# Rank scatter of 8 x 2,048 rows: 256 rows a batch copied from HBM to HBM by two more queues, in place of passing through SBUF

## The chip, the cores and the metric

The kernel runs on one core of a Trainium2 chip. The metric is device time in microseconds. Three runs of the kernel before took 800.44, 800.96 and 801.1 us, median 800.96. One execution was also recorded by the hardware profiler; all views below come from it.

## The reference

The input `x` has 8 batches of 2,048 rows, each of 2,560 float32 values (10,240 bytes). For each batch, 2,048 scores give every row its rank, and row i goes to output row rank(i):

```python
order = np.argsort(scores, axis=1)
ranks = np.argsort(order, axis=1)
out[b_idx, ranks, :] = x
```

So 167.8 MB are read, 167.8 MB are written, and the only arithmetic is the counting of ranks.

## The kernel before, in words

**Ranks.** The rank of a score is the number of smaller scores in its batch, plus the number of equal ones at an earlier index. The scores come in as 8 rows of 2,048 (L114). TensorE transposes them into columns of 128 (L156, `s_col`), so that one column holds one score per partition; for each batch it also broadcasts the 2,048 scores to all partitions (`broadcast`, L177, into PSUM), and VectorE copies them to `s_all` (L215). VectorE then goes through the columns (`count`, L231 to L259): one instruction counts smaller scores from the group's first column on (L246), one counts smaller or equal ones in the columns before the group (L250), one counts equal ones within the group under a mask (L255). All three carry line L237 in the profile. Two additions (L263, L269) and a conversion to integers (L286, `rank_i`) make the ranks of a group.

**Groups.** `GROUPS` (L55) lists groups of rows of a batch as (first row, rows per partition m, direct). Before, there are four groups of 512 rows, m = 4, none direct. `ORDER` (L56) is the order in which VectorE and the bulk queue take them. `BULK` (L59) lists all (batch, group) pairs that aren't direct: 32 before.

**Bulk path.** A group is loaded into one of four SBUF buffers by one DMA (`load`, L105, issued at L108; 128 partitions, m rows each, one contiguous run of m x 10,240 bytes per partition), and written by m indirect DMAs (L340), each of which scatters one row of every partition to the row that `rank_i` names. The first four loads are issued by SP (L115). All else goes through the Pool queue in one hand-written order (L326): for entry k, wait for the scatters of entry k-2, issue the load of entry k+2 into its buffer, wait for the load of k and for its ranks, issue the m scatters.

**Direct path.** The code has a second path, which with the groups of before has no work (`todo`, L292, is empty). For a direct group, TensorE transposes the ranks into a row (L279) and VectorE turns them into byte offsets, (rank + b x 2048) x 10,240, in `rows_i` (`rows_out`, L195); this is done only after the next group's two additions (L273), so that VectorE does not wait for TensorE. SP and ACT take the direct columns in turn (L297). For each column of 128 rows the engine waits for the offsets (L299), loads 16 offsets at a time into registers (L301), and issues one DMA per row, from the row of `x` in HBM straight to its row of the output in HBM (L312), each adding 16 to a semaphore of that engine. At the end SP and ACT wait for all of them (L318). Neither engine has other work after the first loads.

All waits are placed by hand (`Line`); within one engine, instructions run in the order of the code.

Of the kernel before, what the change touches and what calls it, by code (L numbers as in the profile page):

```python
# [40 lines left out]
def kernel(  # L41
# [10 lines left out]

    GROUPS = [(0, 4, False), (512, 4, False), (1024, 4, False), (1536, 4, False)]  # L55
    ORDER = [0, 1, 2, 3]  # L56
    MMAX = max(m for _, m, _ in GROUPS)
    MBULK = max(m for _, m, direct in GROUPS if not direct)
    BULK = [(b, g) for b in range(B) for g in ORDER if not GROUPS[g][2]]  # L59
    NBUF = 4  # L60
    G = 16

    def first_col(g):
        return GROUPS[g][0] // P

# [23 lines left out]
    with tc.tile_critical():  # L89
# [15 lines left out]
        def load(line, k, sem):  # L105
            b, g = BULK[k]
            r, m, _ = GROUPS[g]
            line.eng.dma_start(  # L108
# [42 lines left out]
        pe.after(pl, t_ident)  # L151
        for g, (r, m, _) in enumerate(GROUPS):
            for j in range(m):
# [56 lines left out]
        for b in range(B):  # L210
# [11 lines left out]
            dve.after(dve, t_copied)  # L222
            for g in ORDER:
                r, m, direct = GROUPS[g]
# [63 lines left out]
        if pending is not None:  # L288
# [3 lines left out]
        todo = [  # L292
            (b, g, j) for b in range(B) for g in ORDER if GROUPS[g][2]
            for j in range(GROUPS[g][1])
# [88 lines left out]
```

## Time and profile before

| | before |
|---|---|
| median of 3 runs | 800.96 us |
| the profiled execution | 801.1 us |
| its span, first to last instruction | 799.3 us |
| VectorE busy | 426.3 us, all of it before about 440 us |
| POOL busy | 142.7 us |
| TensorE busy | 29.5 us |
| 128 scatters, each | 0.95 us to issue (median), 40.7 us from issue to landing |
| 28 loads by Pool, each | 0.56 us to issue, 36.1 us from issue to landing |

A span is the time from the first to the last instruction of the execution. The page cuts it into 40 equal slices and gives each engine's busy share in tenths (9 is 90% or more); DMA is the mean share of the core's 16 DMA engines. A queue's share is the time that its packets took, as part of 16 engines' span. The chain that ended last is followed back from the last instruction, at each step to what released it. A row of a tile view gives the shortest, median and longest duration in ns, then the first and last start in us. A packet is the unit in which a DMA engine moves data; the trace records start, queue, duration and size of each.

### The profile page before, as it was taken

What the parts mean: (1) busy time and instruction counts of PE and PEld (TensorE: products, weight loads), DVE (VectorE), ACT (ScalarE), POOL (GpSimd) and SP (SyncE); (2) the same over time, 40 slices, a digit from 0 to 9 for tenths busy, and PEclk for the clock granted to TensorE, in tenths of its full rate; (3) what the DMA queues carried; (4) which work ended last, traced back from release to release, by engine and by line L of the source; (5) the groups of instructions that cost most, each with busy time, mean ns of one, the idle gap of its engine ahead of it and who ended that gap; (6) DMA issues with size and microseconds to landing.
All of it is one profiled execution on the core that took longest, in us unless ns stands there. A gap on an engine that the chain in (4) does not pass through costs nothing.

```text
span 799.3 us, 1452 instructions
## 1 busy us (share of the span) xinstructions
PE 29.5 (4%) x144; PEld 26.6 (3%) x144; DVE 426.3 (53%) x834; POOL 142.7 (18%) x165
## 2 busy tenths in 40 slices
PE   3001000010010010100000000000000000000000
PEld 3001000010010010100000000000000000000000
DVE  6999999999999999999998000000000000000000
POOL 1302222102222012220222201222111222104100
PEclk9555555555555555555555555555555555555555
DMA  9999999999999999999999999999999999999993
GB/s 378 427 414 448 397 431 431 444 422 423 419 432 431 439 425 409 425 434 435 421 427 422 437 430 434 426 422 430 437 441 424 425 424 434 434 440 423 420 429 154
DMA packets 23066, 335.71 MB, mean 420 GB/s; under 512 B 2568, under 2 KB 2568, under 8 KB 2568
## 3 DMA queue, kind: packets, MB, share of 16 engines
q0 software_dynamic: 22464, 314.58, 92.5%
q1 hardware_dynamic: 592, 21.04, 6.3%
q14 instruction: 9, 0.07, 0.0%
q8 instruction: 1, 0.02, 0.0%
HBM read 167.84 MB, written 167.77 MB: 420 GB/s over the span
## 4 chain that ended last, share of the span: by engine, by line
DMA 54%; DVE 34%; POOL 4%; issue 3%; PE 1%; POOLq 0%; SPq 0%
DMA out_dram<-x,rank_i 49%; DVE trash L237 31%; DMA x<-in_x_dram 4%; POOL out_dram L340 4%; DVE s_all L215 2%; POOL x L108 1%; PE ps_all L177 0%; DVE rank L263 0%; DVE rank L269 0%; DVE rank_i L286 0%; DMA s_in<-in_scores_dram 0%; PE ps_col L156 0%; POOLq L28 0%; DVE s_col L164 0%; SPq L378 0%
## 5 line engine op out<-in xcount | busy, mean ns | idle before, releaser
L237 DVE TENSOR_SCALAR_CACHE_REDUCE trash<-s_all,s_col 128x1536 bf16<-128x1536 f32 (+3 forms) x224 | 312.4, 1426 | 0.3
L340 POOL DMA_INDIRECT out_dram<-x,rank_i x128 | 124.2, 970 | 91.8 <-issue 37.8
L108 POOL DMA_DIRECT2D x<-in_x_dram x28 | 15.8, 564 | 526.1 <-DMA out_dram<-x,rank_i 279.6
L237 DVE SCALAR_TENSOR_TENSOR trash<-s_all,s_col,mask 128x512 bf16<-128x512 f32 x128 | 95.9, 749 | 0.0
L177 PE MATMUL ps_all<-ident,s_col 128*128 128x128 f32 x128 | 27.5, 404 | 303.0 <-DVE s_all L215 302.6
L177 PEld LDWEIGHTS ps_all<-ident,s_col 128*128 128x128 f32 x128 | 24.6, 216 | 305.5 <-DVE s_all L215 305.0
L215 DVE COPY s_all<-ps_all 128x512 f32<-128x512 f32 x32 | 20.2, 684 | 1.8 <-PE ps_all L177 1.5
L237 DVE DVE_READ_ACCUMULATOR trash<-s_all,s_col 128x1 f32 x224 | 18.3, 82 | 0.0
L237 DVE DVE_READ_ACCUMULATOR trash<-s_all,s_col,mask 128x1 f32 x128 | 10.4, 81 | 0.0
L286 DVE CAST rank_i<-rank 128x4 int32<-128x4 f32 x32 | 5.6, 176 | 1.1
L263 DVE TENSOR_TENSOR rank<-acc,acc 128x4 f32<-128x4 f32 x32 | 5.2, 164 | 1.1
L269 DVE TENSOR_TENSOR rank<-rank,acc 128x4 f32<-128x4 f32 x32 | 5.2, 162 | 1.1
L164 DVE COPY s_col<-ps_col 128x128 f32<-128x128 f32 x1 | 0.3, 291 | 4.7 <-PE ps_col L156 4.7
L156 PE MATMUL ps_col<-ident,s_in 8*128 8x8 f32 x16 | 2.1, 264 | 3.8 <-DMA s_in<-in_scores_dram 3.8
L156 PEld LDWEIGHTS ps_col<-ident,s_in 8*128 8x128 f32 x16 | 2.0, 212 | 3.8 <-DMA s_in<-in_scores_dram 3.8
L137 POOL TENSOR_SCALAR_AFFINE_SELECT mask<-mask 128x512 f32<-128x512 f32 x2 | 1.2, 626 | 0.0
L120 POOL MEMSET mask<- 128x1024 f32 x1 | 1.0, 952 | 0.0
L149 DVE MEMSET acc<- 128x128 f32 x1 | 0.2, 165 | 1.1 <-SPq L89 1.1
L119 POOL MEMSET ident<- 128x128 f32 x1 | 0.2, 204 | 0.5 <-ACTq L378 0.5
L123 POOL TENSOR_SCALAR_AFFINE_SELECT ident<-ident 128x128 f32<-128x128 f32 x1 | 0.3, 284 | 0.0
L367 POOL MEMSET const-float32-0.0<- 128x1 f32 x1 | 0.1, 98 | 0.3 <-issue 0.3
L367 POOL MEMSET const-uint8-127<- 128x1 uint8 x1 | 0.1, 118 | 0.0
(2 smaller groups left out, 0.2 us busy)
## 6 DMA issues: line engine op xcount, KB each, us to landing
x<-in_x_dram POOLq DMA_DIRECT2D x28, 5120.0 KB, 36.1
x<-in_x_dram SPq DMA_DIRECT2D x4, 5120.0 KB, 35.1
out_dram<-x,rank_i POOLq DMA_INDIRECT x128, 40.7
s_in<-in_scores_dram SPq DMA_DIRECT2D x1, 64.0 KB
```

The lines of the kernel that those rows point to most:

```text
L108: line.eng.dma_start(out=xb[k % NBUF][:, :m * D], in_=x[b, r:r + P * m, :].rearrange("(p j) d -> p (j d)", j=m),).then_inc(sem, 16)
L120: t_ones = pl.did(nc.gpsimd.memset(mask[:], 1.0))
L123: nc.gpsimd.affine_select(out=ident[:], in_=ident[:], pattern=[[-1, P]], compare_op=OP.not_equal, fill=1.0, base=0, channel_multiplier=1,)
L137: nc.gpsimd.affine_select(out=part, in_=part, pattern=[[0, MMAX], [-1, P]], compare_op=OP.is_ge, fill=0.0, base=-half, channel_multiplier=1,)
L156: nc.tensor.transpose(out=ps_col[:, B * c:B * (c + 1)], in_=s_in[:, r + j:r + m * P:m], identity=ident[:B, :B],)
L177: nc.tensor.transpose(out=ps_all[:, P * c:P * (c + 1)], in_=s_col[:, c, b:b + 1].to_broadcast([P, P]), identity=ident[:],)
L215: nc.vector.tensor_copy(out=s_all[:, 512 * q:512 * (q + 1)], in_=ps_all[:, 512 * q:512 * (q + 1)],)
L237: how.pop("do")(out=trash[i][:, :P * (hi_c - lo_c)], in0=s_all[:, P * lo_c:P * hi_c], accum_out=acc[which][:, col:col + 1], **how,)
L263: nc.vector.tensor_tensor(out=rank[:, cols], in0=acc[0][:, cols], in1=acc[1][:, cols], op=OP.add)
L269: nc.vector.tensor_tensor(out=rank[:, cols], in0=rank[:, cols], in1=acc[2][:, cols], op=OP.add)
L286: nc.vector.tensor_copy(out=rank_i[:, cols], in_=rank[:, cols])
L340: nc.gpsimd.indirect_dma_start(out=out_flat, out_offset=bass.IndirectOffsetOnAxis(ap=rank_i[:, col:col + 1], axis=0), in_=xb[i][:, j * D:( ...
```

## The change

The last group of 512 rows of each batch is split in two: rows 1536 to 1791 stay in the bulk path with two rows per partition, and rows 1792 to 2047 become a direct group, again two columns of 128 rows. The direct group is the second in order within each batch.

```diff
-    GROUPS = [(0, 4, False), (512, 4, False), (1024, 4, False), (1536, 4, False)]
-    ORDER = [0, 1, 2, 3]
+    GROUPS = [(0, 4, False), (512, 4, False), (1024, 4, False), (1536, 2, False), (1792, 2, True)]
+    ORDER = [0, 4, 1, 2, 3]
```

By this, 2,048 of 16,384 rows go by the direct path: 1,024 one-row DMAs issued by SP and 1,024 by ACT, with 64 batches of 16 register loads on each. `BULK` still has 32 entries; 8 of them load and scatter half as much, so there are 32 loads and 112 scatters, where there were 128. The counts of equal scores in the two small groups (L255) cover 256 scores where they covered 512. Nothing else of the code differs; the waits and issues of the direct path are those described above.

## The prediction

> **What bounds the kernel now.** I read first the page's engine line and slices, then its DMA part, then the chain that ended last.
>
> ```profile
> span 799.3 us, 1452 instructions
> ...
> PE 29.5 (4%) x144; PEld 26.6 (3%) x144; DVE 426.3 (53%) x834; POOL 142.7 (18%) x165
> ...
> DMA  9999999999999999999999999999999999999993
> ...
> DMA packets 23066, 335.71 MB, mean 420 GB/s; under 512 B 2568, under 2 KB 2568, under 8 KB 2568
> ...
> q0 software_dynamic: 22464, 314.58, 92.5%
> q1 hardware_dynamic: 592, 21.04, 6.3%
> ...
> HBM read 167.84 MB, written 167.77 MB: 420 GB/s over the span
> ...
> DMA out_dram<-x,rank_i 49%; DVE trash L237 31%; DMA x<-in_x_dram 4%; POOL out_dram L340 4%; DVE s_all L215 2%; POOL x L108 1%; PE ps_all L177 0%; DVE rank L263 0%; DVE rank L269 0%; DVE rank_i L286 0%; DMA s_in<-in_scores_dram 0%; PE ps_col L156 0%; POOLq L28 0%; DVE s_col L164 0%; SPq L378 0%
> ```
>
> The DMA engines are full in every slice but the last; 92.5% + 6.3% = 98.8% of the 16 engines' span is packet time. The chain names DVE for 31%, but only because it follows the last releaser: DVE ends near 440 us of 799, while DMA is as full before that as after. So the bound is the sum of packet times on the engines, and the change is priced by packet time. The stretches 200:300 and the tail (columns: stretch, length, busy PE, PEld, DVE, POOL, clock, DMA share, GB/s):
>
> ```profile
> 200.00:300.00 100.00, 7.35 (x32) 6.55 (x32) 99.14 (x194) 17.77 (x20) 0.52 1.01 429
> ...
> 784.00:788.00 4.00, 0.00 (x0) 0.00 (x0) 0.00 (x0) 0.00 (x0) 0.50 0.52 220
> 788.00:792.00 4.00, 0.00 (x0) 0.00 (x0) 0.00 (x0) 0.00 (x0) 0.50 0.20 84
> ```
>
> A share of 1.01: no gap for a cheaper issue or wait to close. In the tail some engines run dry some 10 us before others; I leave it as it is.
>
> **Packet prices.** The trace's packet records: 10,240 B (a scattered row) 385 ns, 40,960 B (four loaded rows) 1,514 ns, 8,192 B (scores) 307 ns, a 4 B semaphore packet 9 ns. One line fits: (1514 - 385) / 30720 = 0.03675 ns per byte, plus 8.7 ns a packet.
>
> **Removed.** 256 rows of 8 batches = 2,048 rows leave the bulk. Each cost a quarter of a load packet, 1514/4 = 378.5 ns, and a scatter packet, 385 ns, spread over 16 engines: 763.5/16 = 47.7 ns per engine and row, x 2048 = 97.7 us. The last bulk group of a batch now loads two rows per partition: 20,480 B cost 761 ns against 757 for half of 1,514, 64 such packets per engine, +0.3 us; 16 scatters' semaphores go, -0.1. Net **-97.6 us**.
>
> **Added on the DMA engines.** 2,048 one-row copies HBM to HBM. Nothing in the trace shows one, neither its pieces nor its price. Pieces: each of the 32 loads posts 16 semaphore packets, one per engine used, so I take 16 pieces of 640 B, each followed by its own semaphore packet (9 ns): per row, every engine does one such pair. Price of the 640 B from below: the line gives 8.7 + 0.03675 x 640 = 32.2 ns, pair 41.2, x 2048 = 84.4 us. From above: a read packet and a write packet, 64.4, pair 73.4, 150.4 us. In between: bytes twice, overhead once: 8.7 + 47.0 = 55.7, pair 64.7, **132.6 us**. I take the last. In every packet of before one side is HBM and the other SBUF, so 420 to 430 GB/s is the rate to and from HBM as much as the rate of the engines; a copy has both sides there, and the nearest rows for its two sides are a load's share and a scatter's share. Break-even is 47.7 - 9 = 38.7 ns for the 640 B packet. A semaphore after every packet, not after eight, may also cost more than 9 ns; the share of 1.01 shows no stall at before's rate.
>
> In the Trainium skill, "DMA: Bandwidth & Descriptors", section "Latency and other measured facts", the entry on HBM row pitch speaks against this change: copies between HBM tensors in 16 KiB pieces ran at 207 to 214 GB/s per direction at best. As an estimate, 214/16 = 13.4 GB/s per engine makes 640 B 48 ns, the pair 65.5 and the total 838 us, where the one-way price of the rows would give 788; no row here shows such a copy yet.
>
> **Who issues them, and when they fit.** SP and ACT issue 1,024 each, after DVE has the ranks (L299). The order of lines and the chain by time:
>
> ```profile
> 61.73 2.50 DVE s_all L215 x4
> ...
> 115.46 2.50 DVE s_all L215 x4
> ```
>
> A batch takes DVE 53.7 us. Group 0's counts end at 23 us; two direct columns take 6.3 us (half of the 12.9 of four), and the byte offsets are written only after the next group's ranks (12.9): about 43 us, then every 53.7 us, the last near 419. Issue cost, from the tile view of x:
>
> ```profile
> L340 POOL DMA_INDIRECT out_dram<-x,rank_i x128: 946/952/1373, 24.0 to 760.5; - x128
> L108 POOL DMA_DIRECT2D x<-in_x_dram x28: 563/563/573, 67.8 to 720.6; - x28
> L108 SPq DMA_DIRECT2D x<-in_x_dram x4: 354/426/895, 1.5 to 2.8; - x4
> ```
>
> An SP issue took 354 to 895 ns, median 426; 1,024 of them end between 43 + 362 = 405 and 43 + 916 = 959 us. Loading 16 registers per 16 rows comes on top, with no row to price it; I take the median and up to 0.3 us for the load, 787 us at most, inside the span. The Trainium skill, "Runtime: NRT & Kernel Launch", section "Instruction fetch mechanics", puts a register load from HBM at some 200 ns; by that estimate the last row is issued at 43 + 1024 x 0.63 = 688 us, though here the registers come from SBUF.
>
> Two queues on one engine alternate packet by packet. From 30 to 50 us, while SP's loads and Pool's scatters compete, the DMA view has:
>
> ```profile
> q1 hardware_dynamic: 176, 6.55, 76.2%
> q0 software_dynamic: 176, 1.64, 19.4%
> ```
>
> Equal packets, four times the bytes. So each of the two new queues gets one row per bulk packet. Pool's queue has 112 scatters and 28 loads of 8 packets per engine: 1,120 turns, mean (896 x 385 + 168 x 1514 + 56 x 761)/1120 = 573 ns; with two pairs beside it, 703 ns. 1,024 turns take 720 us: rows end near 763 us, before the bulk. They fit, narrowly.
>
> **At no cost.** DVE gains a transpose wait and eight offset writes, and loses half of 32 equality counts (749 ns each): it has 360 us to spare behind DMA. Group 1's ranks come 6.3 us later (42 instead of 36 us): four loads of 18.4 MB and group 0's scatters, 5.2 MB, fill the queue to about 56 us. POOL issues 16 scatters fewer, 16 us of an engine busy 18%. The new waits (L299, L318) stand on SP and ACT, behind which only row copies are queued. If that cover went, group 1's lateness would cost 6 us at the start.
>
> **Sum.** The profiled execution took 801.1 us (span 799.3 and 1.8 around it), 0.14 above the median of the three runs. 801.1 - 97.6 + 132.6 = **836 us**. By the two bounds of the copy: 788 and 854.
>
> **Rivals.**
> 1. *The copy costs one way* (41.2 ns a pair): **788 us**, faster. For it: the line fits loads and scatters alike, so the engine may be what limits, whatever the ends are. Against: no packet with both ends in HBM.
> 2. *Issue sets the end, much slower*: if a row costs SP or ACT over (836 - 43)/1024 = 0.774 us, rows are still being issued when the bulk is done, with the engines nearly idle. At SP's longest, 0.895, **960 us**. For it: unpriced register loads and addresses; against: the median of 426 ns.
> 3. *HBM traffic is the limit, not packets*: 335.6 MB are read and written before and after; **801 us**, no change. Against: single slices reach 444 GB/s.
> 4. *The row isn't cut in 16.* Whole rows spread evenly: (385 + 9)/16 = 24.6 ns, 50 us, **754 us**. All on one engine: 2048 x 394 ns = 807 us beside that engine's 691 of bulk, some **1,500 us**.
>
> **Chances.** Forecast 0.47 (own range 820 to 880: a pair price of 57 to 73 ns, up to 86 if the semaphores stall); rival 1 0.27; rival 2 0.14; rival 3 0.06; rival 4 0.03 and 0.03. Faster by over 0.2%, about what a measurement of this kernel can tell from none: 0.27 + 0.03 = 0.30; within it 0.06; slower 0.47 + 0.14 + 0.03 = 0.64. The range, 780 to 890, holds the forecast, rivals 1 and 3, and rival 2 up to 0.825 us a row; out of it are rival 4 and most of rival 2.
>
> **What would show it.** Some 65,500 more small packets, half of 4 B: 640 B is right. The copy packet's duration: 32 ns is rival 1, 56 the forecast. The DMA share at 1.0 to the end says packets bound; a long end with a low share and SP or ACT still issuing says rival 2. DMA full and a higher rate with a shorter span says 1 or 4. The forecast is wrong if copies overlap their two sides, or if a semaphore after each packet stops an engine.

## The result and the profile after

The changed kernel takes 1,021.22 us (median of 4 runs, 1,021.06 to 1,021.42) where the kernel before took 800.87 us (800.44 to 801.1): a ratio of 1.275, 95% interval 1.273 to 1.277. The forecast was 836 us, with a range up to 890. The sign was right, but for a reason that turned out wrong; the time is far outside, and the mechanism is another than the one forecast.

The page of the changed kernel:

```profile
span 1019.7 us, 5693 instructions
...
DMA  9999999999999999999999999999822111111111
GB/s 387 412 430 422 425 407 419 423 423 425 424 427 414 427 423 417 418 423 407 404 428 425 394 410 423 425 413 420 347 39 30 29 29 28 29 29 29 29 28 23
DMA packets 86331, 315.14 MB, mean 309 GB/s; under 512 B 35080, under 2 KB 67848, under 8 KB 67848
...
q0 software_dynamic: 20160, 275.26, 63.4%
q1 hardware_dynamic: 33360, 28.97, 9.6%
q10 hardware_dynamic: 32768, 10.55, 5.1%
```

The DMA row shows where the time went: full for 28 slices, then over a quarter of the span at one or two tenths, 29 GB/s. Before, the engines were full to the last slice. q10 is ACT's queue, new here: 32,768 packets, that is 1,024 rows x 16 pieces and as many semaphores. So a row is cut into 16 pieces of 640 B, as assumed. The stretches (stretch, length, busy PE, PEld, DVE, POOL, clock, DMA share, GB/s):

```profile
700.00:730.00 30.00, 0.00 (x0) 0.00 (x0) 0.00 (x0) 1.91 (x2) 0.50 1.02 416
730.00:740.00 10.00, 0.00 (x0) 0.00 (x0) 0.00 (x0) 0.00 (x0) 0.50 0.61 211
740.00:760.00 20.00, 0.00 (x0) 0.00 (x0) 0.00 (x0) 0.00 (x0) 0.50 0.23 40
800.00:900.00 100.00, 0.00 (x0) 0.00 (x0) 0.00 (x0) 0.00 (x0) 0.50 0.17 29
```

The bulk runs out between 730 and 750 us; in the kernel before it did so between some 780 and 792. The change thus did win 40 to 50 us on the bulk, and lost 270 us behind it, in which only row copies run. Two questions follow: why were so many rows left when the bulk was done, and why are they slow then?

The second first. The rows of SP's issues, up to 735 us, from 100 to 700 us and from 800 to 900 us, and of its register loads in the last stretch (count, then shortest/median/longest ns, first and last start):

```profile
L312 SPq DMA_DIRECT2D out_dram<-in_x_dram x640: 3/588/3695, 43.3 to 734.5; - x160
...
L312 SPq DMA_DIRECT2D out_dram<-in_x_dram x532: 154/586/3695, 100.1 to 699.7; - x178
...
L312 SPq DMA_DIRECT2D out_dram<-in_x_dram x138: 517/547/806, 799.9 to 898.5; - x138
L312 SPq MOVE out_dram<-in_x_dram x137: 29/29/29, 800.5 to 898.4; - x137
...
L301 SPq TENSOR_LOAD <-rows_i x9: 968/973/977, 806.2 to 899.0; - x9
```

Alone, SP issues 138 rows in 100 us, 0.72 us a row: 547 ns for the DMA, 29 for a move of its address, 973/16 = 61 for its share of a register load, and some 85 ns in which no record stands. Beside the bulk it issued 532 rows in 600 us, 1.13 us a row, and single issues were held for up to 3.7 us. By 735 us SP had issued 640 rows; the other 384 at 0.72 us make 276 us: 1,011, and the last issue stands at 1,012.9.

Now the first question. The DMA view of the changed kernel from 200 to 300 us (queue: packets, MB, share of the 16 engines):

```profile
q0 software_dynamic: 2888, 40.30, 94.4%
q10 hardware_dynamic: 2888, 0.93, 3.7%
q1 hardware_dynamic: 2888, 0.93, 3.7%
```

Three queues, the same number of packets to the last one, though one moves 40 MB and the others 0.93 each. The counts hold the 4 B semaphore packets. Equal totals alone would also come from turns of several packets each; but in the packet records, from 100 to 400 us and over all 16 engines together, the running counts of the three queues are never more than 6 apart. So turns are taken packet by packet, **and a semaphore is a packet**: a row copy takes two turns of its queue, 640 B and 4 B. Pool's queue has 140 DMAs of 9 packets per engine, 1,260 turns, which let 630 rows per queue through, not 1,024. (SP's 640 are a few more: from 500 to 700 us Pool's queue had 5,739 packets against 5,924 and 5,912, so it must have stood empty now and then.)

### The profile page after: what moved, and what is told of

The parts are those of the page before. It is cut to its first block, busy times and chain, and to the rows that moved or that the text cites. A ratio compares the mean times of both kernels' runs of the same rounds, so it can differ in the third digit from the quotient of the medians.

```text
span 1019.7 us, 5693 instructions
## 1 busy us (share of the span) xinstructions
PE 34.2 (3%) x152; PEld 28.8 (3%) x152; DVE 421.2 (41%) x858; POOL 129.6 (13%) x149
## 3 DMA queue, kind: packets, MB, share of 16 engines
q10 hardware_dynamic: 32768, 10.55, 5.1%
## 4 chain that ended last, share of the span: by engine, by line
DMA 53%; DVE 11%; POOL 3%; issue 2%; PE 1%; POOLq 0%; SPq 0%
DMA out_dram<-x,rank_i 50%; DVE trash L237 10%; DMA x<-in_x_dram 3%; POOL out_dram L340 2%; POOL x L108 1%; DVE s_all L215 1%; PE ps_all L177 0%; PE ps_col L156 0%; DVE rank L263 0%; DVE rank L269 0%; DVE rank_i L286 0%; POOL mask L137 0%; POOL mask L120 0%; POOLq L28 0%; DVE rows_i L200 0%
## 5 line engine op out<-in xcount | busy, mean ns | idle before, releaser
L237 DVE TENSOR_SCALAR_CACHE_REDUCE trash<-s_all,s_col 128x1536 bf16<-128x1536 f32 (+4 forms) x224 | 312.0, 1423 | 0.3
L340 POOL DMA_INDIRECT out_dram<-x,rank_i x112 | 111.0, 991 | 91.4 <-issue 34.5
L237 DVE SCALAR_TENSOR_TENSOR trash<-s_all,s_col,mask 128x512 bf16<-128x512 f32 (+1 forms) x128 | 86.7, 678 | 0.0
L279 PE MATMUL ps_row<-ident,rank 128*2 128x128 f32 x8 | 3.0, 373 | 156.5 <-DVE rank L269 141.7
L269 DVE TENSOR_TENSOR rank<-rank,acc 128x4 f32<-128x4 f32 (+1 forms) x40 | 6.5, 163 | 1.4
L263 DVE TENSOR_TENSOR rank<-acc,acc 128x4 f32<-128x4 f32 (+1 forms) x40 | 6.5, 162 | 1.4
L286 DVE CAST rank_i<-rank 128x4 int32<-128x4 f32 (+1 forms) x32 | 6.0, 189 | 0.8
L200 DVE TENSOR_SCALAR rows_i<-ps_row 2x128 int32<-2x128 f32 x8 | 2.2, 271 | 0.0
```

Source lines behind the costliest of these rows:

```text
L200: nc.vector.tensor_scalar(out=rows_i[:m, b, :], in0=ps_row[:m, :P], scalar1=float(b * N), scalar2=float(ROW), op0=OP.add, op1=OP.mult,)
L237: how.pop("do")(out=trash[i][:, :P * (hi_c - lo_c)], in0=s_all[:, P * lo_c:P * hi_c], accum_out=acc[which][:, col:col + 1], **how,)
L263: nc.vector.tensor_tensor(out=rank[:, cols], in0=acc[0][:, cols], in1=acc[1][:, cols], op=OP.add)
L269: nc.vector.tensor_tensor(out=rank[:, cols], in0=rank[:, cols], in1=acc[2][:, cols], op=OP.add)
L279: nc.tensor.transpose(out=ps_row[:m, :P], in_=rank[:, cols], identity=ident[:])
L286: nc.vector.tensor_copy(out=rank_i[:, cols], in_=rank[:, cols])
```

## The experiments

The theory: turns cap the rows beside the bulk; the rest runs at the price of issue. The rivals: the issue itself is slow while other engines work; the copy itself is dear; HBM is the limit.

**Loads cut by row: more turns for the rows.** Each load becomes one DMA per row of a partition; packets of 10,240 B take the place of 40,960 B ones.

```diff
...
-            line.eng.dma_start(
-                out=xb[k % NBUF][:, :m * D],
-                in_=x[b, r:r + P * m, :].rearrange("(p j) d -> p (j d)", j=m),
-            ).then_inc(sem, 16)
+            rows = x[b, r:r + P * m, :].rearrange("(p j) d -> p j d", j=m)
+            for j in range(m):
+                line.eng.dma_start(
+                    out=xb[k % NBUF][:, j * D:(j + 1) * D], in_=rows[:, j, :]
+                ).then_inc(sem, 16)
...
```

The lines left out count the loads, so that Pool waits for all of a buffer's.

> The changed kernel, but each bulk load is cut into one DMA per row of a partition, so that its packets are 10,240 B instead of 40,960 B; the rows, the scatters and the row copies are the same. Theory (packets take turns): on every DMA engine the three queues take turns packet by packet, the 4 B semaphore packets counted, so a row copy needs two turns of its queue, and the number of packets in Pool's queue sets how many row copies get done beside the bulk. Pool's queue has 112 scatters and 98 loads here, 9 packets each per engine, 1,890 turns where the changed kernel had 1,260. That lets 940 of a queue's 1,024 rows through before the bulk ends near 763 us, at 0.77 us a row where the changed kernel took 1.13; the other 84 follow at the 0.72 us that a row takes alone, 60 us. Expected 825 us, between 800 and 850. Rival (the issue of a row takes 1.1 us as long as Pool and VectorE are busy, whatever the packets): the time stays at 1,000 to 1,040 us. Rival (a row copy itself is dear): the bulk ends later than 763 us, and the time is above 870 us.

Measured: 868.5 us, ratio to before 1.084 (1.080 to 1.087), 153 us less than the changed kernel with more packets, not fewer. Its DMA view, from 200 to 300 us, then from 500 to 700:

```profile
q0 software_dynamic: 4270, 38.84, 91.9%
q1 hardware_dynamic: 4270, 1.38, 5.5%
q10 hardware_dynamic: 4159, 1.34, 5.4%
...
q0 software_dynamic: 8259, 75.19, 91.4%
q1 hardware_dynamic: 7478, 2.41, 4.9%
q10 hardware_dynamic: 7411, 2.39, 4.8%
```

Half as many turns again, and 4,270/2/16 = 133 rows in 100 us, 0.75 us a row, where the changed kernel had 90. The rival of slow issue falls, and so does that of the dear copy, for the bulk ran out near 763 us, as expected. The time is 18 us above the range I gave: later on the row queues miss a tenth of their turns, and at 763 us SP had issued 887 rows where 940 were expected. The 53 more that were left, at 0.72 us, make 38 of the 43 us by which the time missed 825. Why turns were missed is not shown. A likely reason is that they come nearly as fast as a row can be issued: beside the bulk a register load took SP 1.86 us (median from 500 to 700 us) where it took 0.97 alone, so that a queue could now and then stand empty.

**128 rows a batch.** The last group keeps 384 rows in the bulk, and 128 go direct.

```diff
-    GROUPS = [(0, 4, False), (512, 4, False), (1024, 4, False), (1536, 2, False), (1792, 2, True)]
+    GROUPS = [(0, 4, False), (512, 4, False), (1024, 4, False), (1536, 3, False), (1920, 1, True)]
```

> The changed kernel with 128 direct rows a batch instead of 256 (the last group is 384 bulk rows of three per partition and 128 direct rows). Theory: 512 rows per queue need 1,024 turns, Pool's queue has 148 DMAs with 9 packets per engine each, 1,332 turns, so all row copies are done near 615 us, beside the bulk, and only the packets' sum counts: 801.1 - 48.9 for the removed rows + 1,024 pairs of 32 + 9 ns = 42, that is 794 us, just faster than before. If a copied byte costs twice (pair 65 ns): 801.1 - 48.9 + 66 = 818 us. Rival (a row takes 1.13 us to issue while the bulk runs): 512 x 1.13 + 43 = 622 us, also beside the bulk, so the time doesn't tell this rival apart; the run settles the price of a copy.

Measured: 794.8 us, ratio to before 0.9928 (0.9914 to 0.9942). The same change at half its size takes 0.7% less than the kernel before: little, but with an interval clear of 1. From its page:

```profile
span 793.0 us, 3589 instructions
...
DMA  8999999999999999999999999999999999999980
...
q10 hardware_dynamic: 16384, 5.28, 2.7%
```

The rows were done beside the bulk: SP issued its last at 601 us, ACT, whose first column comes a batch later, at 658. The engines are full to 770 us. From 775 to 785 the share is 0.06, about one engine of 16, so the last 20 us are not packets that all engines share, and it is in part luck that a sum of packet times, 794, came within 1 us. The price doesn't rest on that; q10 gives it: 2.7% of 793 us are 21.4 us per engine for 512 rows, 41.8 ns a pair. That is the one-way price of the first rival (41.2), not my 64.7.

**The same bytes in big packets.** One DMA per column of 128 rows, to a spare tensor; the direct rows are left out of the output.

```diff
-            for q in range(P // G):
...
+            rows = x[b, r:r + P * m, :].rearrange("(p j) d -> p j d", j=m)
+            line.eng.dma_start(
+                out=spare[P * n:P * (n + 1), :], in_=rows[:, j, :]
+            ).then_inc(s_rows[line], 16)
...
```

> The changed kernel, but each column of 128 direct rows is copied by one DMA of 128 packets of 10,240 B to a spare tensor in HBM, without its ranks: the direct rows are left out of the output. SP and ACT issue 8 such DMAs each, where they issued 1,024, and post 128 semaphore packets each instead of 16,384. Theory: with few packets and few issues the copies fit beside the bulk; a copy costs one way, 2,048/16 x 385 ns = 49 us, and the time is 801.1 - 97.6 + 50 = 754 us. If a copied byte costs twice: 801.1 - 97.6 + 98.6 = 802 us. If HBM itself is the limit at some 430 GB/s read plus written: 801 us as well, but with the DMA share below 1.

Measured: 750.3 us, ratio 0.937 (0.936 to 0.939). Its page:

```profile
span 750.1 us, 1481 instructions
...
q10 hardware_dynamic: 1152, 10.49, 3.4%
...
HBM read 167.84 MB, written 167.77 MB: 447 GB/s over the span
```

3.4% of 750 us over 64 packets per engine is 398 ns for 10,240 B, with both ends in HBM; the median of the packet records is 385 ns, that of a scattered row. And HBM took 447 GB/s over the whole span: the rival in which HBM traffic is the limit falls. The 97.6 us for the removed work fit as well: the sum made of them was 754.

**One queue in place of two.** 128 rows a batch, as in the run of that name, all issued by SP.

```diff
...
-            line, name = ((sp, ENG.SP), (act, ENG.Activation))[n % 2]
+            line, name = sp, ENG.SP
...
```

> 128 direct rows a batch, all 1,024 issued by SP, none by ACT: the same bytes, packets and semaphores as with both queues. Theory: one queue needs 2,048 turns and Pool's queue has 1,332, so SP gets about 660 rows through by the end of the bulk near 765 us; the other 360 follow at 0.72 us each, 260 us: 1,025 us, between 980 and 1,070. Rival (issue alone limits, 0.72 us a row from 43 us on): 43 + 737 = 780 us, so the end is that of the bulk, near 800 us. Rival (1.13 us of issue a row while and after the bulk): 43 + 1,024 x 1.13 = 1,200 us.

Measured: 1,010.9 us in one run, against 794.8 with the same bytes and packets in two queues. Its DMA view from 200 to 300 us, and its stretches:

```profile
q0 software_dynamic: 2796, 41.78, 97.7%
q1 hardware_dynamic: 2796, 0.90, 3.6%
```

```profile
740.00:760.00 20.00, 0.00 (x0) 0.00 (x0) 0.00 (x0) 0.00 (x0) 0.50 0.89 360
760.00:780.00 20.00, 0.00 (x0) 0.00 (x0) 0.00 (x0) 0.00 (x0) 0.50 0.16 35
780.00:900.00 120.00, 0.00 (x0) 0.00 (x0) 0.00 (x0) 0.00 (x0) 0.50 0.08 15
```

Equal counts again, and a tail at half the rate of two queues. Without contention a row would be issued every 0.72 us and all would be done by 780; neither that nor 1,200 came out.

**No ranks.** Fixed addresses in a spare tensor, so no register loads and no moves; the direct rows are left out of the output.

```diff
-            for q in range(P // G):
...
+            for i in range(P):
+                row = r + m * i + j
+                line.eng.dma_start(
+                    out=spare[n, ROW * i:ROW * (i + 1)], in_=x_bytes[b, row, :]
+                ).then_inc(s_rows[line], 16)
...
```

> The changed kernel, but the 2,048 row copies go to fixed rows of a spare tensor in HBM: no register loads and no moves of an address on SP and ACT; the direct rows are left out of the output. Same number of copies, packets and semaphores. Theory: beside the bulk a row still needs two of the turns that Pool's packets set, 1.13 us, so some 645 of 1,024 rows per queue are done by the end of the bulk; only the 380 that are left get cheaper, by the 61 ns of a register load's share and the 29 ns of a move, from 0.72 to some 0.60 us: 1,021 - 45 = 975 us, between 955 and 990. Rival (the register loads on SP and ACT set the pace of the rows throughout): 1,024 x 0.58 + 43 = 637 us for the rows, so the time is the packets' sum, near 790 us. Rival (the pace in the bulk is the issue itself, 1.1 us): 1,000 us or more.

Measured: 988.3 us in one run. SP's issues from 100 to 700 us and from 800 to 960:

```profile
L303 SPq DMA_DIRECT2D spare<-in_x_dram x525: 489/788/3492, 99.7 to 699.6; - x175
...
L303 SPq DMA_DIRECT2D spare<-in_x_dram x249: 488/597/690, 799.9 to 959.4; - x125
```

Beside the bulk nothing changed: 525 rows in 600 us, 1.14 us a row, register loads or not. So they don't set the pace there. Alone a row takes 160/249 = 0.64 us, not the 0.60 expected: the DMA instruction itself got longer, 597 ns instead of 547, which I can't explain. The 384 rows left over at some 0.08 us less make 31 of the 33 us of difference.

**Fewer rows.** Only 96 of each column's 128 rows are copied, 768 per queue; the other 512 rows of the output are left out.

```diff
-            for q in range(P // G):
+            for q in range(6):
...
```

> The changed kernel, but only 96 of the 128 rows of each direct column are copied, 768 per queue; the other 512 rows of the output are left out. The bulk is as in the changed kernel. Theory: Pool's 1,260 turns let some 645 rows per queue through by the end of the bulk, which falls near 741 us whatever the number of rows beyond; the other 123 follow at 0.72 us, 89 us: 835 us, between 815 and 850. If the end went with the number of rows copied rather than with what is left over after the bulk (768/1024 of the 220 us lost): 966 us.

Measured: 835.4 us in one run. The loss goes with the rows left over after the bulk, not with the rows copied: 1,024 rows a queue cost 1,021 us, 768 cost 835, and 512 (with more bulk beside them) 795, below the kernel before.

## Why the prediction was wrong, point by point

- *What bounds the kernel*: right, and it holds for the changed kernel up to 730 us.
- *Removed, 97.6 us*: right. In the packet records the bulk's loads, scatters and semaphores add up to 789.1 us per engine before and 690.8 after, 98.3 less.
- *Pieces of 640 B with a semaphore each*: right.
- *Price of a pair, 64.7 ns*: wrong. It was 41.0 in the changed kernel (3.7% of 100 us over 90.25 rows) and 41.8 with 128 rows, the lower bound. My argument, that a copy has both its sides in HBM and pays for both, was an inference from where the bytes of before went, and no row carried it. The first rival read the same line of prices as a property of the engine and was right. By the forecast's own sum this price makes 788 us, faster than before, had the rows fitted; no run shows that. So the sign, slower, was right by luck: the reason given for it, a dear copy, was wrong.
- *"Each of the two new queues gets one row per bulk packet"*: **this step failed**, and the 233 us between 788 and the measured 1,021 lie here. (The miss against 836 is smaller, 185 us, because the pair was priced 48 us too high in all.) The view that I quoted for it, 176 packets against 176, contains 16 semaphore packets in each count. Read with them it says that packets of any size alternate; I read it as data packets alternating, put 1,120 turns against 1,024 rows and wrote "they fit, narrowly". With semaphores it is 1,260 turns against 2,048, and 384 of SP's 1,024 rows were left at 735 us.
- *Issue*: median of 426 ns plus up to 0.3 us for the register load; measured 0.72 us in all, when rows run alone. The total was right by luck, for its parts were not: 547 ns for the DMA, 61 for the register load, and over 0.1 us that the sum did not have. The limit of 0.774 is not passed alone. The second rival's picture is the one that came (engines nearly idle, SP and ACT still issuing), but its cause was not: issue sets the pace only after the bulk, for the rows that turns had kept back.
- *Ranks at 43 us*: the first register load starts at 41.9. The edits at no cost were that: the DMA share shows no hole before 730 us.
- *Semaphores that stall an engine*: not seen; the share stays at 1.02 with a semaphore after every 640 B packet.
- *HBM traffic as the limit (rival 3)*: wrong by the run with big copies. The slices quoted against it reach 448 GB/s, not 444.

One page can be set beside this, in two places. The Trainium skill, "DMA: Bandwidth & Descriptors", section "Queues, rings and completion order", says that an engine goes round its queues and drains a packet of some 9 to 17 descriptors before it switches. The round is what the counts show; the size of a turn is not: it was one packet record here, be it 40,960 B or 4 B, with running counts that stay within 6. The entry on HBM row pitch in the section "Latency and other measured facts", by which I estimated 838 us, did not carry over: a copy of 10,240 B cost 398 ns here, 25.7 GB/s per engine where the estimate had 13.4. But copies were only a fifteenth of the moved bytes (21 of 314.7 MB), and no run had copies alone at full rate.

## What to carry to other kernels

Where several queues are busy, count packets per queue and engine, semaphores included: a queue of small DMAs gets as many packets as the big one, not as much time, so work moved to it is capped by the number of packets of its neighbour. Size the moved share so that it ends with its neighbour (here at most some 640 rows per queue; 512 were run, and won 0.7%); beyond that each row costs its full issue, 0.72 us on its queue, against 41 ns of an engine's time. And a rate read from a view is worth no more than the knowledge of what its count contains.

## What the runs showed of the hardware that I had not expected

- Queues that all have work alternate by single packets, 2,888 each in 100 us, whatever their size; a 4 B semaphore packet takes a turn of its own, though only 9 ns of time.
- Beside the bulk, an HBM-to-HBM copy packet cost no more than a load or a scatter: 32 ns for 640 B and 385 ns for 10,240 B (medians of the records). Behind the bulk, with nothing but row copies running, the 640 B records of the changed kernel took 29 ns in the median but 56 in the mean; no run shows why.
- Cutting loads into smaller packets made this kernel 153 us faster, by giving the other queues more turns.
- One row DMA costs SP 547 ns, and a load of 16 registers from SBUF 0.97 us, when only row copies run.
